# Delta rule in 32x32 blocks: the inversion on 128 GpSimd partitions, sent by GpSimd itself and joined by 32x32 matmuls

## The chip, the cores and the metric

One Trainium2 chip, one core of it. The metric is device time in microseconds of one execution; the median of three executions is given. The profile is one execution taken by the hardware profiler.

## What is computed

The program is a three-layer network over 512 tokens. The change lies in the first layer's mixer, which runs three attention groups and a gated delta rule (8 heads of width 128) beside each other. The delta rule as the reference has it, cut to what matters here:

```python
a_mat = jnp.where(tril_strict, jnp.einsum('nbhid,nbhjd->nbhij', kbeta, kc) * decay_mat, 0.0)
t_mat = lax.linalg.triangular_solve(eye + a_mat, eye, left_side=True, lower=True, unit_diagonal=True)
u = jnp.einsum('nbhij,nbhjd->nbhid', t_mat, vc * bc[..., None])
w = jnp.einsum('nbhij,nbhjd->nbhid', t_mat, kbeta * jnp.exp(gcum)[..., None])
```

The kernel works with chunks of 128 tokens, so each head has four strictly triangular 128x128 matrices, and the inverse of (1 + a) is wanted for each.

## The kernel before

All large products are made in three matmuls from a high and a low part of both operands (`gemm`, line 295), 24 matmuls of 128x512 for a slab of weights. A slab is loaded by SP (line 278) and split by ScalarE (`whi`, line 282) and VectorE (`wlo`, line 286).

`first_mixer` (from line 912) weaves two streams: the eight heads of the delta rule (`dn_head`) and the attention (`attention`, twelve pairs and four mixes). Both are generators; each `yield x` says how much TensorE work, in planned units, was just written. `interleave` always continues the stream that is least far along relative to its total, `DN_T` for the heads and `AT_T` for the attention. Within the heads, the second half of head h-1 is interleaved with the first half of head h, once the three convolutions of head h are written (`heads`). Head 0's second half thus stands among head 1's first half, and head 7's second half stands beside attention alone. This gives the program order; the framework's scheduler makes each engine's order from it at build time, and an engine then runs its instructions strictly in that order. `tc.issue_after(self.last_mm.ins)` keeps the transposes of `t_` (line 587) behind the last large matmul written before them. After the mixer comes `branch`, whose `pB` products need all eight heads.

The part of a head that matters, with its lines:

- Line 540: GpSimd scales `dec`. Line 551: VectorE makes `at`, the transposed triangular matrices of the four chunks, 128x512.
- Lines 560 to 577: the diagonal 16x16 blocks are inverted. SP writes `at` to `blk[0]` in HBM (one DMA) and reads 32 diagonal blocks back, one block on each of 32 partitions (four DMAs). GpSimd runs forward substitution, 15 steps of a product and a subtraction (lines 571 and 573). SP writes the result to the diagonal of `blk[1]` (four DMAs), which was zeroed once, and reads the whole as `t_` (one DMA).
- Line 587: TensorE transposes `t_`, ScalarE copies it to `tt` (line 588).
- Lines 590 to 598: two levels join 16 to 32 and 32 to 64. Each level takes a masked `at` from GpSimd (`xm`, line 555), four 128x128 products (line 547), a copy by ScalarE (line 593), four more products, a subtraction by VectorE (line 595), four transposes (line 496) and a copy by ScalarE (line 597).
- Lines 600 to 610: the last level joins 64 to 128 with 64x64 products on parts of the array (lines 603 and 609).
- Then `kbe`, the recurrence over four chunks, the output norm and the gate. GpSimd multiplies the gate in (line 668). In `attn_mix` GpSimd adds up the groups (line 851).

An fp32 product is two instructions on TensorE in the profile, so four products show as x8; a transpose is one.

Of the kernel before, what the change touches and what calls it, by code (L numbers as in the profile page):

```python
# [22 lines left out]
F32 = mybir.dt.float32  # L23
# [8 lines left out]
P = 128  # L32
# [3 lines left out]
NEG = -1.0e30  # L36
MAGIC = float(0x5F3759DF)

DN_T, AT_T = 280.0, 251.0
DN2 = "cy", "at", "aq", "qd", "kbe", "ktl", "bv"  # L40
S5_T = 150.0
L0_POOL = 10
L0_T = 142.0, 88.0
AHEAD = 90
LEAD = (0, 1)
NR = 6
N0, SK = 4, 2
# [30 lines left out]
def _consts():  # L78
    p = np.arange(P)
    f = np.float32  # L80
    eye = (p[:, None] == p[None, :]).astype(f)
    neg = lambda ok: np.where(ok, f(0), f(NEG)).astype(f)
    c = {}
    c["ident"] = eye
    c["m_up"] = neg(p[:, None] <= p[None, :])
    c["m_lo"] = neg(p[:, None] >= p[None, :])
    c["m_prev"] = neg(p[None, :] >= p[:, None])
    c["m_res"] = neg((p[:, None] // 32 == p[None, :] // 32) & (p[:, None] >= p[None, :]))
    c["tri"] = (p[:, None] <= p[None, :]).astype(f)
    c["half"] = (p[:, None] // 64 == np.arange(2)[None, :]).astype(f)  # L90
    for i in range(7):
        b = 1 << i
        ok = (p[:, None] // (2 * b) == p[None, :] // (2 * b)) & (p[:, None] // b % 2 == 0) & (p[None, :] // b % 2 == 1)
        c[f"lv{i}"] = ok.astype(f)
    x = np.arange(3 + 512)
    c["un1"] = (x[None, :] - 3 == 4 * p[:, None]).astype(f)
    x = np.arange(12 + 512)
    c["un2"] = (x[None, :] - 12 == 16 * (p[:, None] % 32) + p[:, None] // 32).astype(f)
    return c


# [117 lines left out]
class Kern:  # L219
# [230 lines left out]
        self.hb = t("hb")  # L450
        nc.vector.tensor_scalar(self.hb, self.beta, 0.5, None, op0=OP.mult)

    @staticmethod
    def diag(t, c):

        a = t[:, c * P : (c + 1) * P]
        return bass.AP(a.tensor, a.offset, [[16 * S + 16, 8], [S, 16], [1, 16]])

    def dn_head(self, h):

        nc, dl, pa = self.nc, self.dl, self.pa
# [1 line left out]
        def T(tag, dt=F32):  # L463
            return dl.tile([P, S], dt, tag=tag, name=tag, bufs=2 if tag in DN2 else 1)
# [4 lines left out]
        def c4(x):  # L469
            return x.rearrange("p (c n) -> p c n", c=4)  # L470
# [22 lines left out]
        def tokmajor(x):  # L493
            ps = ptile("tmps")
            for c in range(4):
                nc.tensor.transpose(ps[:, c * P : (c + 1) * P], x[:, c * P : (c + 1) * P], self.ident)
            return ps
# [45 lines left out]
        def per_chunk(lhs, rhs):  # L543
            ps = ptile("pcps")
            for c in range(4):
                t = slice(c * P, (c + 1) * P)
                nc.tensor.matmul(ps[:, t], lhs[:, t], rhs[:, t], start=True, stop=True)  # L547
            return ps
# [1 line left out]
        at, aq = T("at"), T("aq")  # L550
        nc.vector.tensor_mul(at, per_chunk(sk, kb), dec)
        yield 0.9
        def masked(i):
            x = T("xm")
            nc.gpsimd.tensor_tensor(c4(x), c4(at), self.mb[f"lv{i}"][:, None, :].to_broadcast([P, 4, P]), op=OP.mult)  # L555
            return x


        blk, eng = self.blk[h % 2], self.sub_engine
        nc.sync.dma_start(blk[0], at)  # L560
        x = self.sm.tile([P, S], F32, tag="sq", name="sub", bufs=2)
        lm = dl.tile([32, 64], F32, tag="lm", name="lm")
        La, Lt = (x[0:32, i * 256 : (i + 1) * 256].rearrange("p (i k) -> p i k", k=16) for i in range(2))
        for c in range(4):
            nc.sync.dma_start(La[8 * c : 8 * c + 8], self.diag(blk[0], c))
        eng.memset(Lt, 0.0)
        eng.memset(x[0:32, 256:512:17], 1.0)
        for j in range(15):
            n, w = 15 - j, j + 1
            m = lm[0:32, 0 : n * w].rearrange("p (i k) -> p i k", k=w)  # L570
            eng.tensor_tensor(m, La[:, j, j + 1 :][:, :, None].to_broadcast([32, n, w]),
                              Lt[:, j, 0:w][:, None, :].to_broadcast([32, n, w]), op=OP.mult)
            eng.tensor_sub(Lt[:, j + 1 :, 0:w], Lt[:, j + 1 :, 0:w], m)
        for c in range(4):
            nc.sync.dma_start(self.diag(blk[1], c), Lt[8 * c : 8 * c + 8])
        tt, t_ = T("tt"), T("t")
        nc.sync.dma_start(t_, blk[1])
        nc.vector.tensor_mul(aq, per_chunk(sk, sq_), dec)
        yield 0.9
        rowmul(qd, sq_, [self.egc[:, c, h : h + 1] for c in range(4)])  # L580
# [2 lines left out]
        nc.vector.tensor_tensor(c4(bv), c4(pv), colb(self.hb), op=OP.mult)  # L583
        yield 0.5
        yield None
        with self.tc.issue_after(self.last_mm.ins):
            ps = tokmajor(t_)
        nc.scalar.copy(tt, ps)
        yield 0.2
        for i in (4, 5):  # L590
            x = masked(i)
            y = T("ty")
            nc.scalar.copy(y, per_chunk(x, t_))
            yield 0.9
            nc.vector.tensor_sub(tt, tt, per_chunk(y, tt))
            yield 0.9
            nc.scalar.copy(t_, tokmajor(tt))
            yield 0.2

        a, b = slice(0, 64), slice(64, 128)  # L600
        ps = ptile("pcps")
# [41 lines left out]
        ot = self.ob[h]  # L643
        nc.scalar.copy(ot, po)
        self.dump(f"o_raw{h}", ot)
        q2 = T("xm")
        nc.scalar.activation(q2, po, AF.Square)
        yield 1.5
        v = dl.tile([P, 4], F32, tag="ov", name="ov")
# [15 lines left out]
        nc.vector.tensor_mul(z, ps, self.rb)  # L665
        nc.scalar.activation(th, z, AF.Tanh, scale=0.5)
        nc.vector.scalar_tensor_tensor(z, th, 1.0, z, op0=OP.add, op1=OP.mult)
        nc.gpsimd.tensor_tensor(ot, ot, z, op=OP.mult)
        yield 5.4


# [137 lines left out]
    def attn_mix(self, j):  # L809

        nc, at, pa = self.nc, self.at, self.pa
        ms = [self.stat[0]]
        for g in (1, 2):

            ps = pa.tile([4, S], F32, tag="aa", name="unps", bufs=2)
            for b in range(4):
                nc.tensor.transpose(ps[:, b * P : (b + 1) * P], self.stat[g][:, b].rearrange("p a h -> p (a h)"), self.ident)
            row = at.tile([4, S], F32, tag="unr", name="unr")
            nc.scalar.copy(self.perm(row, g), self.as_perm(ps, g))
            ps = pa.tile([P, 4, 4], F32, tag="aa", name="unpt", bufs=2)  # L820
            for b in range(4):
                nc.tensor.transpose(ps[:, b, :], row[:, b * P : (b + 1) * P], self.ident[0:4, 0:4])
            t = at.tile([P, 4, 2, 2], F32, tag=f"mst{g}", name=f"mst{g}")
            nc.vector.tensor_copy(t.rearrange("p n a h -> p n (a h)"), ps)
            ms.append(t)
        yield 0.8
        mm = at.tile([P, 4, 2], F32, tag="mm_", name="mm_")
        nc.vector.tensor_tensor(mm, ms[0][:, :, 0], ms[1][:, :, 0], op=OP.max)
        nc.vector.tensor_tensor(mm, mm, ms[2][:, :, 0], op=OP.max)
        es, zz = [], at.tile([P, 4, 2], F32, tag="zz", name="zz")  # L830
        for g in range(3):
            e = at.tile([P, 4, 2], F32, tag=f"es{g}", name=f"es{g}")
            nc.vector.tensor_tensor(e, ms[g][:, :, 0], mm, op=OP.subtract)
            nc.scalar.activation(e, e, AF.Exp)
            es.append(e)
            if g == 0:
                nc.vector.tensor_tensor(zz, e, ms[g][:, :, 1], op=OP.mult)
            else:
                t = at.tile([P, 4, 2], F32, tag="zt", name="zt")
                nc.vector.tensor_tensor(t, e, ms[g][:, :, 1], op=OP.mult)  # L840
                nc.vector.tensor_add(zz, zz, t)
        nc.vector.reciprocal(zz, zz)
        oa = at.tile([P, S], F32, tag="unr", name="oa")
        for g in range(3):
            nc.vector.tensor_mul(es[g], es[g], zz)
            ps = self.half_rows(at, es[g].rearrange("p b e -> p (b e)"))
            if g == 0:
                nc.vector.tensor_mul(oa, self.on[g], ps)
            else:
                nc.vector.tensor_mul(self.on[g], self.on[g], ps)  # L850
                nc.gpsimd.tensor_add(oa, oa, self.on[g])
            yield 0.2
        self.dump(f"oa{j}", oa)
        self.split(oa, self.oah[j], self.oal[j])
# [57 lines left out]
    def first_mixer(self):  # L912
        nc, tc = self.nc, self.tc
        with ExitStack() as c0:
# [4 lines left out]
            with ExitStack() as c1:  # L919
# [22 lines left out]
                    nc.scalar.dma_start(t, self.I["consts"][:, o : o + w])  # L942
                    return t

                for n in ("m_up", "m_res", "m_lo", "m_prev", "lv4", "lv5"):
                    self.mb[n] = dk.tile([P, P], BF, name="b" + n)
                    nc.gpsimd.tensor_copy(self.mb[n], load(n))
                for n in ("tri",):
# [3 lines left out]
                self.on = [at.tile([P, S], F32, name=f"on{g}") for g in range(3)]  # L952
                self.stat = [at.tile([P, 4, 2, 2], F32, name=f"stat{g}") for g in range(3)]
                dram = c1.enter_context(self.pool("blk", 1, bass.MemoryType.DRAM))
                self.blk = [[dram.tile([P, S], F32, name=f"blk{i}{j}") for j in range(2)] for i in range(2)]
                z = self.sm.tile([P, S], F32, tag="sq", name="zsq")
                nc.gpsimd.memset(z, 0.0)
                for i in range(2):
                    nc.scalar.dma_start(self.blk[i][1], z)
                self.sub_engine = nc.gpsimd  # L960
                self.cin = self.dl.tile([P, S + 4], F32, name="cin")
                nc.gpsimd.memset(self.cin[:, 0:4], 0.0)
                self.gqk = at.tile([P, 1], F32, name="gqk")
# [1191 lines left out]
```

## Time and profile before

| | |
|---|---|
| median of 3 runs | 2258.52 us (2255.84 to 2261.11) |
| the profiled execution | 2258.31 us |
| its span, first to last instruction | 2256.5 us |
| mean granted TensorE clock | 0.983 |
| TensorE busy | 2143.0 us, 95% |
| VectorE busy | 1487.9 us, 66% |
| ScalarE busy | 966.1 us, 43% |
| GpSimd busy | 442.5 us, 20%, 616 instructions |

The span is the time from the first to the last instruction on the core; 1.8 us of the execution lie around it. Matmuls overlap in the pipeline, so busy time of TensorE says only when it had something in flight; what a group of matmuls costs is read from the distance of starts.

### The profile page before, as it was taken

How to read it: one execution, taken by the hardware profiler on the slowest of the kernel's cores; microseconds unless marked ns; L12 is line 12 of the kernel's file. 1: busy time of each engine (PE TensorE's matmuls, PEld its weight loads, DVE VectorE, ACT ScalarE, POOL GpSimd, SP SyncE). 2: the span in 40 equal slices, each digit the busy share in tenths (PEclk: the TensorE clock that was granted, in tenths of full speed). 3: DMA queues.
4: the chain of work that ended last, by engine and by line, in shares of the span. 5: the costliest groups of instructions: out<-in, count | busy, mean ns of one | idle time of the engine just before them, and what ended most of it. 6: DMA issues, size and time to landing. Idle time of an engine off the chain costs nothing.

```text
span 2256.5 us, 28801 instructions
## 1 busy us (share of the span) xinstructions
PE 2143.0 (95%) x10718; PEld 1701.1 (75%) x10718; DVE 1487.9 (66%) x2674; ACT 966.1 (43%) x1594; POOL 442.5 (20%) x616
## 2 busy tenths in 40 slices
PE   8999999999999998999897899999999889999997
PEld 6787777777777886665785677788888778888886
DVE  6766766766755456775789878847476567777533
ACT  4434444444443233665464454424334245444321
POOL 0222022022020013101236059600330220000000
PEclk9999999999999998999998999999999999999998
DMA  4221111211212246899221112222232113322332
GB/s 158 67 68 52 67 62 49 80 63 58 72 39 89 92 159 228 305 356 310 89 95 47 29 49 92 94 94 97 84 103 94 47 38 103 103 94 96 96 95 88
DMA packets 83298, 231.13 MB, mean 102 GB/s; under 512 B 18576, under 2 KB 22288, under 8 KB 83152
## 3 DMA queue, kind: packets, MB, share of 16 engines
q1 hardware_dynamic: 78048, 217.02, 29.0%
q0 software_dynamic: 2944, 10.49, 1.4%
q10 hardware_dynamic: 2160, 1.71, 0.3%
q8 instruction: 86, 1.41, 0.3%
q14 instruction: 60, 0.49, 0.1%
HBM read 215.89 MB, written 12.65 MB: 101 GB/s over the span
## 4 chain that ended last, share of the span: by engine, by line
PE 40%; DVE 8%; ACT 2%; issue 1%; POOL 0%; DVEq 0%; POOLq 0%; ACTq 0%
PE mm L295 35%; DVE cvps L1711 2%; DVE wlo L286 1%; DVE fy L1787 1%; PE po L1662 1%; PE psc L1631 0%; PE st L1489 0%; PE gps L1935 0%; PE ppt L1655 0%; ACT whi L282 0%; DVE x L888 0%; DVE t L2044 0%; PE mm L2005 0%; DVE xl L306 0%; PE mm L2006 0%
## 5 line engine op out<-in xcount | busy, mean ns | idle before, releaser
L295 PE MATMUL mm<-xh,whi 128*128 128x512 f32 x1664 | 661.0, 398 | 13.4 <-ACT whi L282 12.9
L295 PE MATMUL mm<-xh,wlo 128*128 128x512 f32 x1664 | 660.3, 397 | 9.3 <-DVE wlo L286 9.2
L295 PE MATMUL mm<-xl,whi 128*128 128x512 f32 x1664 | 659.4, 396 | 7.0 <-DVE xl L303 3.9
L282 ACT CAST whi<-wraw 128x1024 fp32r<-128x1024 f32 (+4 forms) x311 | 301.4, 969 | 518.7 <-PE mm L295 421.7
L286 DVE TENSOR_TENSOR wlo<-wraw,whi 128x1024 fp32r<-128x1024 f32 (+4 forms) x311 | 367.6, 1182 | 127.0 <-ACT whi L282 123.6
L295 PEld LDWEIGHTS mm<-xh,wlo 128*128 128x128 f32 x1664 | 314.7, 189 | 78.3 <-DVE wlo L286 14.8
L295 PEld LDWEIGHTS mm<-xh,whi 128*128 128x128 f32 x1664 | 314.5, 189 | 77.4 <-ACT whi L282 14.2
L295 PEld LDWEIGHTS mm<-xl,whi 128*128 128x128 f32 x1664 | 314.8, 189 | 75.8 <-DVE xl L306 8.0
L1787 DVE SCALAR_TENSOR_TENSOR fy<-fe,par,fy 128x512 f32<-128x512 f32 x176 | 142.0, 807 | 4.0 <-ACT fy L1785 0.9
L295 PE MATMUL mm<-ah,whi 128*128 128x512 f32 x352 | 138.0, 393 | 0.2 <-ACT ah L302 0.2
L295 PE MATMUL mm<-al,whi 128*128 128x512 f32 x352 | 137.3, 391 | 0.0
L295 PE MATMUL mm<-ah,wlo 128*128 128x512 f32 x352 | 137.2, 390 | 0.0
L1782 DVE TENSOR_TENSOR fe<-mm,rb 128x512 f32<-128x512 f32 x88 | 60.3, 688 | 72.0 <-PE mm L295 69.2
L295 PEld LDWEIGHTS mm<-ah,whi 128*128 128x128 f32 x352 | 66.0, 188 | 15.7 <-ACT ah L302 1.5
L295 PEld LDWEIGHTS mm<-al,whi 128*128 128x128 f32 x352 | 66.1, 188 | 14.2 <-DVE al L303 0.4
L295 PEld LDWEIGHTS mm<-ah,wlo 128*128 128x128 f32 x352 | 66.1, 188 | 14.2
L1785 ACT ACTIVATE fy<-fe,par 128x512 f32<-128x512 f32 x88 | 71.9, 817 | 9.6 <-DVE fe L1782 8.9
L302 ACT CAST ah<-fy 128x512 fp32r<-128x512 f32 x44 | 27.4, 623 | 112.6 <-DVE fy L1791 112.5
L1803 DVE TENSOR_TENSOR x<-x,mm 128x512 f32<-128x512 f32 x32 | 22.0, 688 | 79.7 <-PE mm L295 79.7
L555 POOL TENSOR_TENSOR xm<-at,blv 128x512 f32<-128x512 f32 x16 | 19.5, 1222 | 247.0 <-PE pcps L547 201.6
L1124 DVE TENSOR_TENSOR xl<-wraw,xh 128x1024 fp32r<-128x1024 f32 x40 | 48.9, 1223 | 24.6 <-ACT xh L1123 24.0
L1790 ACT ACTIVATE fy<-fy 128x512 f32<-128x512 f32 x44 | 27.9, 634 | 84.9 <-DVE fy L1787 84.9
(746 smaller groups left out, 3646.3 us busy)
## 6 DMA issues: line engine op xcount, KB each, us to landing
wraw<-in_w_up SPq DMA_DIRECT2D x88, 512.0 KB
wraw<-in_w_eu SPq DMA_DIRECT2D x64, 512.0 KB
wraw<-in_w_dn SPq DMA_DIRECT2D x48, 512.0 KB
wraw<-in_w_qkv SPq DMA_DIRECT2D x36, 512.0 KB
wraw<-in_w_ed SPq DMA_DIRECT2D x32, 512.0 KB
wraw<-in_w_g SPq DMA_DIRECT2D x16, 512.0 KB
wraw<-in_w_l SPq DMA_DIRECT2D x16, 512.0 KB
wraw<-in_w_dn SPq DMA_DIRECT2D x16, 448.0 KB
```

What stands on the lines that cost most here:

```text
L282: nc.scalar.copy(hi, raw)
L286: nc.vector.tensor_sub(lo, raw, hi.bitcast(F32))
L295: self.last_mm = nc.tensor.matmul(ps, w, x, start=first and n == 0, stop=last and n == tot - 1)
L302: nc.scalar.copy(hi, src)
L1124: (nc.gpsimd if self.ncv < 5 else nc.vector).tensor_sub(lo, raw, hi.bitcast(F32))
L1662: nc.tensor.matmul(po[:, e, :], pts[e][:, c * P : (c + 1) * P], v1[:, c, h * 64 : h * 64 + 64], start=c == 0, stop=c == b)
L1711: nc.vector.scalar_tensor_tensor(yp, u[:, j : j + S], w(j), yp, op0=OP.mult, op1=OP.add)
L1782: nc.vector.tensor_mul(e[:, 2:], ps, self.rb)
L1785: nc.scalar.activation(y, e[:, 2:], AF.Identity, scale=w(2), bias=self.V(f"l{i}_fcb", f))
L1787: nc.vector.scalar_tensor_tensor(y, e[:, t : t + S], w(t), y, op0=OP.mult, op1=OP.add)
L1790: nc.scalar.activation(c[0], c[0], AF.Silu)
L1803: nc.vector.tensor_add(self.x[m], self.x[m], ps)
```

## The change

A 32x32 block is inverted where a 16x16 block was. GpSimd works on 128 partitions: 16 blocks, eight partitions for each, four rows on a partition. It runs 31 steps of a product and a subtraction on 128 x 4 x i elements, i from 31 down to 1. The blocks go to HBM in eight DMAs of SP and come back in two, each block's columns repeated for its eight partitions; a start matrix (`rows4`) is loaded by SP. The result is written to HBM and read into the diagonal blocks of `t_` by five DMAs that GpSimd itself issues; `t_` is now two fixed tiles, zeroed once. The masked level 16 to 32 goes away. The level 32 to 64 is made of 32x32 products: eight, a copy by ScalarE, and twelve, with results taken from two PSUM banks. The two GpSimd multiplications of lines 668 and 851 go to VectorE; line 540 stays. `DN_T` is 257, and heads 0 and 7 write `yield HOLD` (1.5 units) ahead of the transposes of `t_`.

```diff
-DN_T, AT_T = 280.0, 251.0
+DN_T, AT_T = 257.0, 251.0
+HOLD = 1.5
...
+    c["rows4"] = (x[None, :] % 32 == 4 * (p[:, None] % 8) + x[None, :] // 32).astype(f)
...
-        def masked(i):
-            x = T("xm")
-            nc.gpsimd.tensor_tensor(c4(x), c4(at), self.mb[f"lv{i}"][:, None, :].to_broadcast([P, 4, P]), op=OP.mult)
-            return x
-        blk, eng = self.blk[h % 2], self.sub_engine
-        nc.sync.dma_start(blk[0], at)
-        x = self.sm.tile([P, S], F32, tag="sq", name="sub", bufs=2)
...
-        for c in range(4):
-            nc.sync.dma_start(La[8 * c : 8 * c + 8], self.diag(blk[0], c))
...
-        for j in range(15):
...
-        for c in range(4):
-            nc.sync.dma_start(self.diag(blk[1], c), Lt[8 * c : 8 * c + 8])
-        tt, t_ = T("tt"), T("t")
-        nc.sync.dma_start(t_, blk[1])
+        ab, tb = self.blk[h % 2]
+        eng = self.sub_engine
+        for b in range(4):
+            for i, n in ((1, 32), (0, 16)):
+                o = 32 * b + 16 * i
+                nc.sync.dma_start(bass.AP(ab.tensor, ab.offset + 8192 * i + 64 * n * b, [[16, n], [16 * n, 4], [1, 16]]),
+                                  c4(at)[32 * b : 32 * b + n, :, o : o + 16])
+        La = [None, None]
+        for i, n in ((1, 32), (0, 16)):
+            la = self.sm.tile([P, S], F32, tag="sq", name="la", bufs=2)
+            nc.sync.dma_start(la[:, 0 : 16 * n], bass.AP(ab.tensor, ab.offset + 8192 * i, [[16 * n, 16], [0, 8], [1, 16 * n]]))
+            La[i] = la.rearrange("p (k i) -> p k i", i=16)
+        x = dl.tile([P, 2, P], F32, tag="sub", name="sub")
+        nc.sync.dma_start(x[:, 0, :], self.I["consts"][:, _COFF["rows4"][0] : _COFF["rows4"][0] + P])
+        Lt = x[:, 0, :].rearrange("p (r k) -> p r k", r=4)
+        for i in range(31, 0, -1):
+            m = x[:, 1, 0 : 4 * i].rearrange("p (r k) -> p r k", r=4)
+            eng.tensor_tensor(m, La[i // 16][:, 0:i, i % 16][:, None, :].to_broadcast([P, 4, i]),
+                              Lt[:, :, i][:, :, None].to_broadcast([P, 4, i]), op=OP.mult)
+            eng.tensor_sub(Lt[:, :, 0:i], Lt[:, :, 0:i], m)
+        t_ = self.t_[h % 2]
+        nc.gpsimd.dma_start(tb, x[:, 0, :])
+        for b in range(4):
+            nc.gpsimd.dma_start(c4(t_)[32 * b : 32 * b + 32, :, 32 * b : 32 * b + 32],
+                                bass.AP(tb.tensor, tb.offset + 4096 * b, [[32, 32], [1024, 4], [1, 32]]))
...
         yield None
+        if h in (0, 7):
+            yield HOLD
+        tt, y = T("tt"), T("ty")
         with self.tc.issue_after(self.last_mm.ins):
             ps = tokmajor(t_)
         nc.scalar.copy(tt, ps)
         yield 0.2
-        for i in (4, 5):
-            x = masked(i)
-            y = T("ty")
-            nc.scalar.copy(y, per_chunk(x, t_))
-            yield 0.9
-            nc.vector.tensor_sub(tt, tt, per_chunk(y, tt))
-            yield 0.9
-            nc.scalar.copy(t_, tokmajor(tt))
-            yield 0.2
+        lo, hi = (slice(0, 32), slice(64, 96)), (slice(32, 64), slice(96, 128))
+        ps = [ptile("pcps") for _ in lo]
+        for c in range(4):
+            for p in range(2):
+                nc.tensor.matmul(c4(ps[p])[hi[p], c, 0:32], c4(at)[lo[p], c, hi[p]], c4(t_)[lo[p], c, lo[p]], start=True, stop=True)
+        for p in range(2):
+            nc.scalar.copy(c4(y)[hi[p], :, 0:32], c4(ps[p])[hi[p], :, 0:32])
+        yield 0.3
+        ps = [ptile("pcps") for _ in lo]
+        for c in range(4):
+            nc.tensor.matmul(c4(ps[0])[hi[0], c, 32:64], c4(tt)[hi[0], c, hi[0]], c4(y)[hi[0], c, 0:32], start=True, stop=True)
+            for p in range(2):
+                nc.tensor.matmul(c4(ps[p])[lo[p], c, 0:32], c4(y)[hi[p], c, 0:32], c4(tt)[hi[p], c, hi[p]], start=True, stop=True)
+        nc.scalar.mul(c4(t_)[hi[0], :, 0:32], c4(ps[0])[hi[0], :, 32:64], -1.0)
+        for p in range(2):
+            nc.vector.tensor_scalar(c4(tt)[lo[p], :, hi[p]], c4(ps[p])[lo[p], :, 0:32], -1.0, None, op0=OP.mult)
+        yield 0.5
...
-        nc.gpsimd.tensor_tensor(ot, ot, z, op=OP.mult)
+        nc.vector.tensor_tensor(ot, ot, z, op=OP.mult)
...
-                nc.gpsimd.tensor_add(oa, oa, self.on[g])
+                nc.vector.tensor_add(oa, oa, self.on[g])
...
-                for n in ("m_up", "m_res", "m_lo", "m_prev", "lv4", "lv5"):
+                for n in ("m_up", "m_res", "m_lo", "m_prev"):
...
-                z = self.sm.tile([P, S], F32, tag="sq", name="zsq")
-                nc.gpsimd.memset(z, 0.0)
-                for i in range(2):
-                    nc.scalar.dma_start(self.blk[i][1], z)
+                self.t_ = [self.dl.tile([P, S], F32, name=f"t{i}") for i in range(2)]
+                for t in self.t_:
+                    nc.gpsimd.memset(t, 0.0)
```

## Rows read from the trace of the kernel before

**Rows 1.** Busy us by window (PE, PEld, DVE, ACT, POOL), granted clock, DMA share, GB/s.

```profile
60.00:700.00 640.00, 616.81 (x3684) 491.45 (x3685) 424.40 (x996) 275.51 (x588) 128.65 (x295) 1.00 0.19 62
700.00:750.00 50.00, 50.00 (x219) 40.72 (x218) 24.16 (x24) 14.51 (x19) 3.86 (x3) 1.00 0.28 90
```

**Rows 2.** PE's largest wait, 60 to 700 us: total, times, longest.

```profile
PE rowps L267 <- DVE f L519: 10.1, 8, 1.8
```

**Rows 3.** PE, a product of the two levels, 60 to 700 us: busy, mean ns, idle.

```profile
L547 PE MATMUL pcps<-t,xm 128*128 128x128 f32 x128 | 18.4, 283 | 0.0
```

**Rows 4.** PE in order of time, 274 to 291 us: start, duration, instruction.

```profile
275.88 1.06 PE L547 MATMUL pcps<-kb,sk 128*128 128x128 f32 x8
276.69 0.48 PE L295 MATMUL mm<-xh,whi 128*128 128x512 f32 x1
277.00 0.39 PE L295 MATMUL mm<-xl,whi 128*128 128x512 f32 x1
...
277.91 0.63 PE L496 MATMUL tmps<-ident,tt 128*128 128x128 f32 x4
278.29 0.48 PE L295 MATMUL mm<-xl,whi 128*128 128x512 f32 x1
...
289.02 0.40 PE L295 MATMUL mm<-xh,whi 128*128 128x512 f32 x1
289.36 0.67 PE L603 MATMUL pcps<-t,at 64*64 64x64 f32 x8
289.96 0.50 PE L295 MATMUL mm<-xl,whi 128*128 128x512 f32 x1
290.30 0.40 PE L295 MATMUL mm<-xh,wlo 128*128 128x512 f32 x1
```

**Rows 5.** Head 0 in order of time, from `at` to the transposes of `t_`.

```profile
75.93 0.69 DVE L551 TENSOR_TENSOR at<-pcps,dec 128x512 f32<-128x512 f32 x1 [0.49 <-POOL dec L540]
...
76.65 0.33 SPq L560 DMA_DIRECT2D blk<-at  x1
...
79.22 1.40 SPq L565 DMA_DIRECT2D sub<-blk  x4
...
82.31 0.21 POOL L571 TENSOR_TENSOR lm<-sub 32x15 f32<-32x15 f32 x1 [3.12 <-DMA sub<-blk]
...
95.68 0.21 POOL L573 TENSOR_TENSOR sub<-sub,lm 32x15 f32<-32x15 f32 x1
...
98.73 0.34 SPq L577 DMA_DIRECT2D t<-blk  x1
...
106.45 0.60 PE L496 MATMUL tmps<-ident,t 128*128 128x128 f32 x4
```

**Rows 6.** Head 7 in order of time, from `at` to the 64x64 products.

```profile
613.53 0.69 DVE L551 TENSOR_TENSOR at<-pcps,dec 128x512 f32<-128x512 f32 x1 [0.35 <-PE mm L295]
...
620.87 0.21 POOL L571 TENSOR_TENSOR lm<-sub 32x15 f32<-32x15 f32 x1 [7.38 <-DMA sub<-blk]
...
631.93 0.21 POOL L573 TENSOR_TENSOR sub<-sub,lm 32x15 f32<-32x15 f32 x1
...
643.99 0.66 PE L496 MATMUL tmps<-ident,t 128*128 128x128 f32 x4
...
659.84 0.68 PE L603 MATMUL pcps<-t,at 64*64 64x64 f32 x8
```

**Rows 7.** A wide step of the substitution, in order of time.

```profile
211.71 0.31 POOL L573 TENSOR_TENSOR sub<-sub,lm 32x64 f32<-32x64 f32 x1
```

**Rows 8.** DMAs that GpSimd issues in a later stage, as a group.

```profile
L1270 POOL DMA_INDIRECT big<-h2d,ti x16 | 17.0, 1063 | 132.8 <-PE mm L1409 109.1 <-DVE ovt L1228 10.3 <-DVE hw L1273 8.1
```

**Rows 9.** What SP's queue waited for, 50 to 700 us: total, times, longest.

```profile
SPq L575 <- POOL sub L573: 63.3, 8, 14.0
```

**Rows 10.** Head 1, `dec` on GpSimd and the transposes of `t_`, in order of time.

```profile
114.49 1.04 POOL L540 TENSOR_TENSOR dec<-dec,rqk 128x512 f32<-128x512 f32 x1 [4.63 <-ACT dec L539]
...
186.35 0.60 PE L496 MATMUL tmps<-ident,t 128*128 128x128 f32 x4
```

More of the change, by code (lines that the diff above doesn't have):

```diff
@@ L98, in _consts @@
     c["un2"] = (x[None, :] - 12 == 16 * (p[:, None] % 32) + p[:, None] // 32).astype(f)
+    x = np.arange(P)
+    c["rows4"] = (x[None, :] % 32 == 4 * (p[:, None] % 8) + x[None, :] // 32).astype(f)
     return c
@@ L451, in dn_scalars @@
         nc.vector.tensor_scalar(self.hb, self.beta, 0.5, None, op0=OP.mult)
[L453 to L457, printed above, removed]
     def dn_head(self, h):
@@ L552, in dn_head @@
         yield 0.9
-        def masked(i):
-            x = T("xm")
-            nc.gpsimd.tensor_tensor(c4(x), c4(at), self.mb[f"lv{i}"][:, None, :].to_broadcast([P, 4, P]), op=OP.mult)
-            return x
-        blk, eng = self.blk[h % 2], self.sub_engine
-        nc.sync.dma_start(blk[0], at)
-        x = self.sm.tile([P, S], F32, tag="sq", name="sub", bufs=2)
-        lm = dl.tile([32, 64], F32, tag="lm", name="lm")
-        La, Lt = (x[0:32, i * 256 : (i + 1) * 256].rearrange("p (i k) -> p i k", k=16) for i in range(2))
@@ L564, in dn_head @@
-        for c in range(4):
-            nc.sync.dma_start(La[8 * c : 8 * c + 8], self.diag(blk[0], c))
-        eng.memset(Lt, 0.0)
-        eng.memset(x[0:32, 256:512:17], 1.0)
-        for j in range(15):
[L569 to L573, printed above, removed]
@@ L645, in dn_head @@
         self.dump(f"o_raw{h}", ot)
-        q2 = T("xm")
+        q2 = T("ty")
         nc.scalar.activation(q2, po, AF.Square)
@@ L954, in first_mixer @@
                 dram = c1.enter_context(self.pool("blk", 1, bass.MemoryType.DRAM))
-                self.blk = [[dram.tile([P, S], F32, name=f"blk{i}{j}") for j in range(2)] for i in range(2)]
-                z = self.sm.tile([P, S], F32, tag="sq", name="zsq")
-                nc.gpsimd.memset(z, 0.0)
-                for i in range(2):
-                    nc.scalar.dma_start(self.blk[i][1], z)
+                self.blk = [[dram.tile([P, P], F32, name=f"blk{i}{n}") for n in (0, 1)] for i in range(2)]
                 self.sub_engine = nc.gpsimd
+                self.t_ = [self.dl.tile([P, S], F32, name=f"t{i}") for i in range(2)]
+                for t in self.t_:
+                    nc.gpsimd.memset(t, 0.0)
                 self.cin = self.dl.tile([P, S + 4], F32, name="cin")
```

## The prediction

> **What bounds the kernel now.** I read the table of windows first. From 60 to 700 us, where heads and attention are woven, TensorE is busy 616.8 of 640 us at a granted clock of 1.00; VectorE has 424, ScalarE 276, GpSimd 129, and the DMA engines 19% [rows 1]. Next I read TensorE's waits there: the largest is 10.1 us in eight pieces, for a small VectorE chain that the change leaves alone [rows 2]. So at most 23 us of this stage are idle, and the stage gets shorter by what TensorE no longer has to issue. Behind it TensorE is busy 50 of 50 us with 219 large matmuls, 0.228 us each [rows 1]; what follows the mixer is only moved earlier. Last I followed heads 0 and 7 in order of time, since the result of GpSimd's substitution has least room there [rows 5, 6].
>
> **What leaves TensorE.** Durations overlap, so I count distances of starts. Four 128x128 products (x8) stand 0.81 us before the next large matmul, and that one then takes 0.31 to its successor and not 0.228: 0.89 us a group, 0.101 for each instruction inside [rows 4]. The two levels have four such groups a head (128 instructions in 8 heads for the first product of both levels, and as many for the second) [rows 3]: 3.56 us. Four transposes take 0.38 plus the same 0.08, twice: 0.92 us [rows 4]. A head loses 4.48 us, eight heads 35.8 us.
>
> **What TensorE gets.** Eight and twelve 32x32 products, 40 instructions a head. No row shows one. The nearest is the 64x64 group: 0.60 us for eight, 0.075 each; with both neighbours, 289.02 to 290.30 less two steps of 0.228, it costs 0.82, so 0.22 lies around the group [rows 4]. The ends for a 32x32 instruction: half of 0.075, if it goes by columns, is 0.037; the 0.101 of a 128-wide one is the most. I take 0.05, nearer the row it is next to than a full halving, because consecutive ones use different rows and columns of the array. With two times 0.22 around: 2.44 us a head, 19.5 in all (ends 1.92 and 4.48, so 15.4 and 35.8). TensorE saves 35.8 - 19.5 = 16.3 us, with ends 20.4 and 0.
>
> The 0.22 us around a 64x64 group, against 0.08 around a 128x128 one, speaks against small tiles [rows 4]. [...]
>
> **VectorE and ScalarE.** VectorE loses sixteen 128x512 subtractions and gets sixteen 128x512 products or sums from lines 668 and 851, at 0.69 us like `at` [rows 5]: 11 us each way, and it idles 216 of 640 us [rows 1]. ScalarE loses four copies a head and gets two or three narrower ones. Nothing; if their cover went, both would still be no busier than now. The masks, their loads and the zeroing of HBM at the start go, two memsets come, all on GpSimd and ScalarE's queue ahead of the first `dec`: nothing.
>
> **GpSimd and its queue.** A substitution step took 0.21 us for 15 elements and 0.31 for 64 [rows 5, 7]: 0.18 us plus 2.0 ns an element. The old 30 instructions have 1360 elements, 8.1 us; they took 11.3 in head 7 and 13.6 in head 0 [rows 5, 6], so 0.105 to 0.18 us an instruction go between and beside them. The new 62 have 3968 elements: 19.1 us plus 6.5 to 11.3, so 25.6 to 30.4; I take 27, as head 7 is closer to an undisturbed one. This is 16 us a head more, beside TensorE.
>
> [...]
>
> Before GpSimd starts: 5.7 us from the end of `at` to the first step now. Eight stores at 0.35 us (1.40 for four) instead of one add 2.5, two loads instead of four take off 0.7 [rows 5]: 7.4 us. The `rows4` load needs nothing of `at`. After GpSimd: now 2.8 us to the issue of `t_` and about 2.6 to land, the time from the store of `at` to the loads that wait for it [rows 5]; 5.4. GpSimd's own DMAs cost it 1.06 us each to issue in another stage [rows 8]: 1.06, 2.6 to land, 4 x 1.06 and 2.6: 10.4 us (ends 5.4 and 10.4). From `at` to `t_` it was 24.7 us and will be 44.8, with ends 38.4 and 48.2.
>
> SP's queue is passed: the four stores that waited 63 us for GpSimd, with weight loads behind them, leave it [rows 9]. That gains nothing while no large wait of TensorE is for weights [rows 2]. GpSimd's queue now holds `dec` of the next head behind these 45 us. Between head 1 and later ones there are 70 us or more from `dec` to the use of `t_` (114.5 to 186.4) [rows 10], so six heads hide it all. What shows is at heads 0 and 7.
>
> **Heads 0 and 7.** `t_` was there at 101.3 and used at 106.45 in head 0; head 7 used it at 644.0, 29.8 us after `at` [rows 5, 6]. The 531 planned units fill some 640 us, 1.2 us a unit. `HOLD` puts 1.5 units of head 1 and 2.9 of attention ahead in head 0, 5.3 us, and 1.5 units in head 7, 1.8 us. So `t_` is 121.4 - 111.8 = 9.6 us late in head 0 and 659.0 - 645.8 = 13.2 in head 7. On the other side, the two levels took 15.8 us from the transposes to the 64x64 products [rows 6]; the new one has 2.4 us of products and three short copies, some 5.5. What follows in head 7 is thus about 3 us late. In head 0 GpSimd also comes to `dec` of head 1, now at 114.5, only some 3 us later [rows 10]. TensorE's order already lays other work between dependent groups (a 15.8 us chain with 4.5 us of work in it cost next to no idle time [rows 2, 6]), so I take 5 us of idle time for both heads; ends 0 and, if nothing lies in between, 9.6 + 13.2 = 23.
>
> **Sum.** -16.3 + 5 = -11.3 us against the profiled execution's 2258.3 (span 2256.5 plus 1.8 around it; the median of the runs is 0.2 above it): **2247 us**.
>
> **Rivals.** First, cheap products and no new wait: 0.037 us an instruction and `t_` covered: -20.4, 2238 us. For it: small parts of the array overlap; TensorE's few waits now. Against: 0.22 us around each group does not shrink. Second, nothing to be seen: 32x32 products cost as much as 128-wide ones (0 saved), or waits of 12 to 20 us take the saving back: 2254 to 2262 us, written as 2258. For it: 64x64 ones cost three quarters of 128-wide ones, not a half. Third, slower: TensorE stands at the transposes of `t_` in heads 0 and 7 for the whole lateness, 23 us for 16.3 saved: +6.7, 2265 us. It decides where the order holds less than 16 us of other work ahead of them in both heads together. For it: the arithmetic of the last part, with five DMAs in a row on GpSimd. Against: `HOLD` is a handle for just this place, and products of the next stage, which need no head, can fill head 7.
>
> **Chances.** Forecast 0.50, first rival 0.22, second 0.16, third 0.12. Within 0.2%, or 4.5 us, is what a measurement can hardly tell from no change. Faster by more: 0.50 + 0.22 = 0.72; same 0.16; slower 0.12. The range runs from just below the first rival, 2236, to the upper part of the second, 2261; it leaves out the third and a little below.
>
> **What would show it.** Head 7's 64x64 products should start near 649 us instead of 659.8 [rows 6], with TensorE's idle time up to there some 5 us above what it was. In the groups, 16 and 24 small products with starts 0.05 apart show the saving right; 0.1 apart shows it wrong. Sixty-two steps of GpSimd in 25.6 to 30.4 us, and `t_` landing some 45 us after `at`, show the lateness. A wait of TensorE's transposes for a DMA of 5 us or more in heads 0 and 7 shows the third rival; idle time elsewhere in the weave, on `dec` above all, would make the prediction wrong in a way not counted here.

## The result, and the profile after

The changed kernel takes **2298.22 us** (median of 4 runs, 2297.67 to 2299.41), the kernel before in the same comparison 2257.72 us: a ratio of 1.0174 (95% interval 1.016 to 1.0187). The forecast was 2247 us, with a range up to 2261. It is slower by 40 us; the profiled execution has a span of 2295.9 us.

The table of windows says where. Each row is a stretch, with the busy time of PE, PEld, DVE, ACT and POOL, the granted clock, the DMA share and GB/s. The stretch runs from 60 us to the first product of the stage behind the weave: 682.15 us before, 722.84 us after. The kernel before:

```profile
60.00:682.00 622.00, 598.89 (x3607) 477.09 (x3608) 411.82 (x980) 267.91 (x576) 127.35 (x294) 1.00 0.19 62
```

The changed kernel:

```profile
60.00:722.00 662.00, 592.34 (x3604) 463.17 (x3605) 409.30 (x997) 259.13 (x570) 229.47 (x544) 0.95 0.18 59
```

The weave is 40.7 us longer; what follows takes 1573.1 us where it took 1574.4. TensorE idles 662 - 592.3 = 69.7 us instead of 23.1, and its busy time has hardly fallen, at a clock of 0.95 instead of 1.00. So 46.6 us of new idle time are the first thing to explain. TensorE's waits (total, times, longest) answer to [rows 2]:

```profile
PE tmps L493 <- DMA t<-blk: 21.6, 2, 14.2
PE orps L270 <- DVE ory L667: 8.3, 7, 3.4
PE hrow L699 <- ACT hx L696: 8.1, 2, 7.9
PE qst L736 <- ACT q L733: 8.1, 3, 7.6
PE po L815 <- ACT pt L804: 7.3, 1, 7.3
PE mm L298 <- ACT whi L285: 6.9, 2, 6.6
```

Two kinds are new. One is the wait for `t_`, twice. The other is a single long stop in each of four groups, always for ScalarE: 7.58, 7.29, 6.59 and 7.95 us before 263.43, 349.31, 434.16 and 606.05 us, 29.4 us in all. Both kinds together are 51.0 us; the small waits got 4.4 us shorter.

**The four stops.** One of them, followed back through three engines. TensorE in order of time (start, duration, instruction, idle before it):

```profile
263.43 1.11 PE L736 MATMUL qst<-ident,q 128*128 128x128 f32 x4 [7.58 <-ACT q L733]
```

ScalarE did `q` (L733) late because the conversion of weights ahead of it in its order was late:

```profile
261.80 1.04 ACT L285 CAST whi<-wraw 128x1024 fp32r<-128x1024 f32 x1 [11.86 <-DMA wraw<-in_w_qkv]
262.75 0.63 ACT L733 ACTIVATE q<-k 128x512 f32<-128x512 f32 x1
```

Those weights were asked for at 257.73 us, right behind another load. SP's queue in order of time:

```profile
230.71 0.36 SPq L281 DMA_DIRECT2D wraw<-in_w_dn  x1
257.33 0.36 SPq L565 DMA_DIRECT2D sub<-in_consts  x1
257.73 0.43 SPq L281 DMA_DIRECT2D wraw<-in_w_qkv  x1
```

For 26 us SP issues nothing. It stands at L565, the load of `rows4` into `sub` for the *next* head. There is one `sub` tile; the load has to wait until the head before has left it, and the last to read it is GpSimd's store of its result (L573), issued at 255.39. SP's waits (total, times, longest), to set against [rows 9]:

```profile
SPq L565 <- DMA blk<-sub: 160.2, 7, 26.8
```

The other three stops go the same way: ScalarE's conversions at 347.72, 433.06 and 602.33 us had waited 7.7, 15.0 and 10.6 us for weights that SP asked for right behind the load of `rows4` at 343.34, 428.33 and 598.10. But not each of the seven waits stops TensorE. In order of time they are 22.4, 14.1, 26.2, 25.0, 23.4, 26.8 and 22.1 us; the third, fourth, fifth and seventh are the ones before the four stops. Behind the longest, which ended at 521.58, TensorE was still at work on weights it had, and stood for 0.30 us here and 0.53 us a little later:

```profile
526.55 0.50 PE L298 MATMUL mm<-xh,whi 128*128 128x512 f32 x1 [0.30 <-ACT whi L285]
```

So it is not the length of such a wait alone that decides, but also how much work TensorE has at that place before it needs the weights queued behind.

**`t_` in heads 0 and 7.** Head 0 in order of time, to set against [rows 5]. VectorE, then GpSimd:

```profile
74.25 0.69 DVE L548 TENSOR_TENSOR at<-pcps,dec 128x512 f32<-128x512 f32 x1 [0.15 <-PE pcps L544]
...
82.49 0.48 POOL L569 TENSOR_TENSOR sub<-la,sub 128x124 f32<-128x124 f32 x1 [9.53 <-DMA la<-blk]
...
114.12 0.20 POOL L571 TENSOR_TENSOR sub<-sub 128x4 f32<-128x4 f32 x1
114.63 0.79 POOL L573 DMA_DIRECT2D blk<-sub  x1 [0.31 <-POOL sub L571]
116.98 2.23 POOL L575 DMA_DIRECT2D t<-blk  x4 [1.55 <-DMA blk<-sub]
```

and TensorE:

```profile
123.13 1.09 PE L493 MATMUL tmps<-ident,t 128*128 128x128 f32 x4 [7.36 <-DMA t<-blk]
124.14 0.63 PE L598 MATMUL pcps<-t,at 32*32 32x32 f32 x8
...
125.30 0.63 PE L298 MATMUL mm<-xl,whi 128*128 128x512 f32 x1
125.73 0.63 PE L298 MATMUL mm<-xh,wlo 128*128 128x512 f32 x1
126.15 1.05 PE L802 MATMUL ppt<-ident,pe 128*128 128x128 f32 x4
127.14 0.44 PE L598 MATMUL pcps<-t,at 32*32 32x32 f32 x8
```

From the end of `at` to the use of `t_` are 48.2 us; head 7 has 14.19 us of waiting, and its transposes start at 689.67 instead of the 643.99 of [rows 6].

**The clock behind a stop.** In the rows above, two large matmuls start 0.43 us apart where 0.228 is usual, and four transposes take 1.09 instead of 0.60 us. Windows of the changed kernel around four of the stops, with an undisturbed one among them, and at the end the 10 us right behind the stop of head 7:

```profile
258.00:275.00 17.00, 11.57 (x45) 9.57 (x46) 10.28 (x23) 5.51 (x7) 1.99 (x4) 0.80 0.41 135
275.00:343.00 68.00, 64.28 (x413) 50.35 (x411) 43.30 (x102) 27.57 (x70) 27.36 (x64) 1.00 0.14 46
343.00:360.00 17.00, 10.38 (x56) 7.91 (x57) 8.63 (x24) 6.73 (x12) 2.17 (x4) 0.80 0.34 120
600.00:618.00 18.00, 11.95 (x56) 9.15 (x56) 9.63 (x20) 7.16 (x19) 0.76 (x2) 0.72 0.33 117
684.00:722.00 38.00, 28.92 (x176) 22.66 (x177) 15.44 (x51) 13.87 (x30) 2.42 (x5) 0.69 0.10 31
690.00:700.00 10.00, 10.00 (x80) 6.74 (x79) 2.51 (x15) 3.16 (x9) 0.00 (x0) 0.50 0.00 0
```

In the four windows with a stop the granted clock is 0.69 to 0.80, in the undisturbed one 1.00, and from 690 to 700 us, where TensorE is busy all the time, 0.50. Right behind the four stops it is 0.50 as well (264 to 266, 349 to 351, 434 to 436 and 606 to 608 us), and 1.00 again from 268 to 275, 353 to 360, 438 to 445 and 612 to 618 us. So a stop is paid for twice.

### The profile page after: what moved, and what is told of

It reads as the page before. It is cut to its first block, busy times and chain, and to the rows that moved or that the text cites. A ratio compares the mean times of both kernels' runs of the same rounds, so it can differ in the third digit from the quotient of the medians.

```text
span 2295.9 us, 29008 instructions
## 1 busy us (share of the span) xinstructions
PE 2134.7 (93%) x10718; PEld 1685.3 (73%) x10718; DVE 1485.0 (65%) x2690; ACT 954.4 (42%) x1586; POOL 543.2 (24%) x863
## 3 DMA queue, kind: packets, MB, share of 16 engines
q10 hardware_dynamic: 1584, 1.06, 0.2%
## 4 chain that ended last, share of the span: by engine, by line
PE 39%; DVE 8%; ACT 2%; issue 1%; POOL 0%; DVEq 0%; ACTq 0%; POOLq 0%
PE mm L298 35%; DVE cvps L1723 2%; DVE wlo L289 1%; DVE fy L1799 1%; PE po L1674 1%; PE psc L1643 0%; PE st L1501 0%; PE gps L1947 0%; ACT whi L285 0%; PE ppt L1667 0%; DVE t L2056 0%; PE mm L2017 0%; PE mm L2018 0%; PE mm L2019 0%; DVE x L900 0%
## 5 line engine op out<-in xcount | busy, mean ns | idle before, releaser
L298 PEld LDWEIGHTS mm<-xh,whi 128*128 128x128 f32 x1664 | 316.2, 190 | 86.9 <-ACT whi L285 23.1
L569 POOL TENSOR_TENSOR sub<-la,sub 128x124 f32<-128x124 f32 (+30 forms) x248 | 102.2, 412 | 102.5 <-DMA la<-blk 83.7
L571 POOL TENSOR_TENSOR sub<-sub 128x124 f32<-128x124 f32 (+30 forms) x248 | 96.4, 389 | 19.4
L537 POOL TENSOR_TENSOR dec<-dec,rqk 128x512 f32<-128x512 f32 x8 | 8.3, 1039 | 293.2 <-ACT dec L536 293.2
```

The costliest lines, as they stand in the source:

```text
L298: self.last_mm = nc.tensor.matmul(ps, w, x, start=first and n == 0, stop=last and n == tot - 1)
L569: eng.tensor_tensor(m, La[i // 16][:, 0:i, i % 16][:, None, :].to_broadcast([P, 4, i]), Lt[:, :, i][:, :, None].to_broadcast([P, 4, i]), o ...
L571: eng.tensor_sub(Lt[:, :, 0:i], Lt[:, :, 0:i], m)
```

## The experiments

Nine kernels, in three groups that each share the runs of the kernel before.

### 1. The start matrix stays in SBUF

```diff
-        nc.sync.dma_start(x[:, 0, :], self.I["consts"][...rows4...])
+        eng.tensor_copy(x[:, 0, :], self.r4)
```

`r4` is loaded once, ahead of the heads, by ScalarE's queue. Nothing else differs.

> The changed kernel, but the start matrix of the substitution is kept in SBUF and GpSimd copies it, so that no load stands in SP's queue waiting for the head before. Theory A (SP is held by the load of the start matrix, with weight loads behind it): the four stops of TensorE near 263, 349, 434 and 606 us, 29.4 us, go, and with them the half clock behind them, an estimate of 9 us from the four windows at a granted clock of 0.72 to 0.80; the two waits for t_ stay at about 21 us. 2298 - 38 = 2260 us, between 2254 and 2268. Theory B (GpSimd is too busy, and whatever waits for it is late in any case): the stops move elsewhere, 2290 us or more. Theory C (the small products or the order of the work cost the time): 2290 or more, with TensorE's busy time and not its idle time up.

Measured: **2257.84 us, ratio 0.9998 (0.9987 to 1.0008)**: the whole 40 us are gone, and it is the time of the kernel before. Window of this kernel, and its largest wait:

```profile
60.00:682.00 622.00, 584.88 (x3606) 459.33 (x3607) 410.95 (x997) 259.29 (x571) 236.75 (x551) 0.97 0.19 62
```

```profile
PE tmps L493 <- DMA t<-blk: 19.5, 2, 14.3
```

The four stops are gone, the two waits for `t_` have stayed, and no wait of SP for `sub` is left. Theory A holds, B and C fall: GpSimd works as long as before, and apart from the two waits for `t_` its 28 us a head hurt through the queue that stood behind it. Against the kernel before, busy time is 14.0 us less and idle time 14.0 us more (37.1 for 23.1).

### 2. A little more work ahead of `t_`

```diff
-DN_T, AT_T = 257.0, 251.0
+DN_T, AT_T = 272.0, 251.0
...
-            yield HOLD
+            yield 4.0 if h == 0 else 14.0
```

on top of the first.

> As the run before, and in addition more planned work ahead of the use of t_ in the first and the last head: 4 and 14 units where it was 1.5 each, with the planned total of the heads raised to 272. Theory A (t_ is simply used too early by the order): the two waits for t_, 21.6 us, fall under 5 us, and some 5 us of half clock go with them: 2235 to 2245 us. Rival: there is no other work left to lay in between in the last head, or what is laid there is missed elsewhere, since attention then ends earlier or later than the heads: within 5 us of the run before.

Measured: 2256.67 us, ratio 0.9987 (0.9975 to 0.9998). The rival's number came. This kernel's waits:

```profile
PE tmps L493 <- DMA t<-blk: 15.4, 1, 15.4
PE tmps L493 <- DVE at L548: 7.3, 1, 7.3
```

In head 7 nothing moved: from the end of `at` to the transposes there were 28.8 us of other work in the first experiment and 27.5 here. I read this as the planner having already filled the time for which it took GpSimd to be busy, so that my 14 units lay inside that. That is not shown; the fifth experiment rests on this reading. In head 0 one wait replaced another: `at` of head 1 needs its `dec`, and that stands behind the substitution on GpSimd.

### 3. Half of the substitution

```diff
-        for i in range(31, 0, -1):
+        for i in range(15, 0, -1):
```

The load of `rows4` is left where the change has it.

> The changed kernel with 15 of the 31 steps of the substitution: the 16 longest, which join the two halves of each 32x32 block, are left out. GpSimd then needs about 9 us a head where it needed 28, and everything that waits for it is some 18 us earlier. Theory A (lateness of GpSimd's result, through SP's queue and through t_): stops for weights and t_ nearly gone, TensorE's idle time from 60 us to the end of the stage back to 25 us or less, 2230 to 2240 us. Theory C (the products themselves or the new order): 2270 or more.

Measured: 2233.39 us, ratio 0.9888 (0.987 to 0.9907), as theory A said. One wait for `t_`, 6.2 us, is left, in head 7. SP still waits at the load, for less time:

```profile
SPq L565 <- DMA blk<-sub: 75.3, 7, 16.0
```

TensorE's longest idle times are now that wait and two of 3.2 and 1.9 us, none of them behind a weight load. So the same wait in the same queue costs nothing while it is 11 us a head on average and 16.0 at most, and 29.4 us of idle time when it is 23 and 26.8. That is how the 63.3 us of [rows 9], 14.0 at most, could be harmless. All the waits up to 16.0 us did no harm; above 22 us four of six did.

### 4. Only the join to 64x64 by small products, in the kernel before

```diff
-        for i in (4, 5):
+        for i in (4,):
...
+        y = T("ty")
+        ... # the two passes of 32x32 products, as in the change
```

> The kernel before, in which only the join of 32x32 blocks to 64x64 is done by 32x32 products; the substitution of 16x16 blocks and the masked join to 32x32 stay. Nothing gets later. It takes two groups of four 128x128 products and one of transposes off each head (2 x 0.89 + 0.46 = 2.24 us, 17.9 in all) and adds 40 small products. Theory A (small products cost what the trace of the changed kernel shows, 10.5 us in all): -7, 2248 to 2252 us. My prediction's size (0.05 each and 0.22 around each group, 19.5 us): +1.6, 2257 to 2261 us.

Measured: **2241.76 us, ratio 0.9923 (0.9906 to 0.9941)**: -17 us, more than either said.

```profile
60.00:667.00 607.00, 590.27 (x3772) 467.83 (x3770) 408.12 (x999) 268.77 (x590) 115.65 (x286) 1.00 0.20 63
```

Busy time falls by 8.6 us and idle time by 6.4, to 16.7. By distances of starts, what left TensorE is 18.3 us and the 320 small instructions take 6.4, which is cheaper still than in the changed kernel (10.5). The number of groups explains it: here they stand in 16 groups, in the changed kernel in 27, and a group takes about 0.4 us in both (see the last section). The 6.4 us less of idle time I had not foreseen; the waits for `f` fell from 10.1 to 5.8 us, and I did not test why.

### 5. Much more work ahead of `t_` in head 7

The diff of the second experiment with `1.5 if h == 0 else 30.0` and a total of 285.5.

> The start matrix in SBUF as before, and 30 planned units instead of 1.5 ahead of the use of t_ in head 7 alone (planned total 285.5). With 14 units the distance from at to the use of t_ in head 7 had stayed 28 us, so the planner had already laid that much there by itself, and 14 units added nothing. Theory A (t_ is 43 us behind at, the order gives it 28): with 30 units the order gives it over 40, the wait of 14.3 us in head 7 falls under 3, and the half clock behind it (0.89 and 0.83 in two stretches of 50 us) goes as well; head 0's 5.2 us stay. 2258 - 11 - 8 = 2239 us, between 2234 and 2245. Rival: what is laid in between is missing behind it, so that the chain of the last head stands bare: within 5 us of 2258.

Measured: **2239.42 us, ratio 0.9909 (0.9895 to 0.9923)**, the number expected.

```profile
60.00:663.00 603.00, 580.95 (x3603) 458.65 (x3604) 410.98 (x997) 256.69 (x569) 244.19 (x551) 0.98 0.20 63
```

Between the end of `at` and the transposes of head 7 TensorE now has 42.3 us of other work. Head 7's wait is 0.3 us, head 0's is 7.1. Idle time is back at 22.1 us; the clock is far below 1.00 only behind head 0's wait (0.67 from 110 to 135 us).

### 6. Somewhat more in head 0 as well

`6.0 if h == 0 else 30.0`, total 290, and `dec` of head 1 by VectorE:

```diff
-        nc.gpsimd.tensor_tensor(c4(dec), c4(dec), rk...)
+        (nc.vector if h == 1 else nc.gpsimd).tensor_tensor(c4(dec), c4(dec), rk...)
```

> As the run before, and 6 units instead of 1.5 in head 0 (planned total 290), with dec of head 1 multiplied by VectorE, since with 4 units in head 0 TensorE had waited 7.3 us for at of head 1, whose dec stands behind the substitution in GpSimd's queue. Theory A: head 0's wait of 5.2 us goes too and nothing takes its place: 3 to 8 us below the run before. Rival: head 0's t_ is still waited for, since the planner already lays there what there is: within 2 us of the run before.

Measured: 2243.34 us, ratio 0.9933 (0.992 to 0.9947), 4 us above the run before: a miss for both. Head 0's wait fell from 7.1 to 4.5 us, but head 7 waits 3.5 us again. That a larger total leaves less attention for the same 30 units can account for 0.8 us of it at most: there are 41.5 us of other work where there were 42.3. The rest is `t_` itself, which came later: the transposes start 45.0 us behind the end of `at`, in the run before 42.6. Why was not tested.

### 7. SP sends instead of GpSimd

On top of the first experiment:

```diff
-        nc.gpsimd.dma_start(tb, x[:, 0, :])
+        nc.sync.dma_start(tb, x[:, 0, :])
...
-            nc.gpsimd.dma_start(c4(t_)...)
+            nc.sync.dma_start(c4(t_)...)
```

> The start matrix in SBUF, but the store of GpSimd's result and the four loads of t_ are issued by SP instead of GpSimd. Theory A (whatever waits for GpSimd in SP's queue holds the weight loads behind it, and 28 us are longer than the buffers cover): SP stands at the store for 20 us a head, and stops of TensorE for weights come back: 2275 to 2300 us. Rival (the stores of before waited 63 us in this queue at no cost, and GpSimd is spared four issues): 2250 to 2262 us.

Measured: **2316.73 us, ratio 1.0254 (1.0237 to 1.027)**; theory A's side, and 17 us beyond it. SP's wait is back, now at the store:

```profile
SPq L573 <- POOL sub L571: 177.3, 8, 25.0
```

and ScalarE waits for weights:

```profile
ACT whi L285 <- DMA wraw<-in_w_qkv: 54.3, 4, 15.4
```

It is the mechanism of the four stops made by another instruction; why it costs 17 us more than I expected was not taken apart. So the clause "GpSimd sends them itself" was not the harmless extra that I took it for: with a substitution of 28 us it is what keeps SP free, and the load of `rows4` gave that away.

### 8. GpSimd does the gate product and the sum again

On top of the first: lines 680 and 863 back on GpSimd.

> The start matrix in SBUF, but the gate product of a head and the addition to oa are GpSimd's again, as in the kernel before. Theory (both are needed late, and GpSimd has room): 2254 to 2264 us, as the kernel with the start matrix in SBUF. Rival (they stand behind up to 28 us of substitution in GpSimd's queue, and push dec and the next substitution back by as much as they take): 2265 us or more, with waits of TensorE or SP for oa.

Measured: 2275.73 us, ratio 1.0075 (1.0059 to 1.0092); the rival's side, some 18 us above the first experiment. From 60 us to the end of the weave (699.5) it has 10.6 us more idle time than that one and 6.4 more busy time at a lower clock, 0.96. GpSimd stood 26.3 us at one sum, waiting for ScalarE, with `dec` of the next head behind it; but that `dec` then waited for ScalarE in its turn:

```profile
190.81 3.85 POOL L863 TENSOR_TENSOR oa<-oa,on 128x512 f32<-128x512 f32 x2 [26.25 <-ACT hx L696]
212.20 1.04 POOL L537 TENSOR_TENSOR dec<-dec,rqk 128x512 f32<-128x512 f32 x1 [17.54 <-ACT dec L536]
```

So the sum did not push this `dec` back, and no wait of TensorE or SP for `oa` shows: the rival has the time right, but its mechanism is not shown. ScalarE waits 16.5 us in four pieces for these sums (8.1 us in three in the first experiment). What made the 18 us stays open. Which of the two operations did it was not tried apart.

### 9. More work in head 0 and head 7 together

`12.0 if h == 0 else 33.0`, total 299, `dec` of head 1 by VectorE, start matrix in SBUF.

> The start matrix in SBUF, 33 planned units ahead of the use of t_ in head 7 and 12 in head 0 (planned total 299), dec of head 1 by VectorE. With 6 units in head 0 the wait had only gone from 7.1 to 4.5 us and head 7 got 3.5 us back, since a larger total leaves less attention for its 30 units. Theory A (t_ is late by the length of the substitution, and enough work in the order hides it): head 0's wait goes below 1 us with the half clock behind it, head 7's stays below 2: 2228 to 2236 us. Rival (the work laid into head 0 and 7 is missing between the dependent steps of the other heads, whose small waits grow): 2238 us or more, with the waits for orps and rowps up.

Measured: **2230.39 us, ratio 0.9872 (0.9848 to 0.9895)**, the fastest of all.

```profile
60.00:654.00 594.00, 575.00 (x3605) 452.93 (x3605) 412.21 (x999) 256.20 (x568) 243.44 (x550) 1.00 0.20 64
```

```profile
PE orps L270 <- DVE ory L667: 9.7, 8, 2.0
PE tmps L493 <- DMA t<-blk: 1.4, 1, 1.4
```

The clock is 1.00 throughout and idle time 19.0 us. With both clocks at 1.00, this row also gives the price of the change in busy time: 598.9 - 575.0 = 23.9 us less work for TensorE.

## Why the prediction was wrong

With that price each kernel's weave adds up, against the kernel before, from the windows:

| us | work | slower clock | idle | weave |
|---|---|---|---|---|
| changed kernel | -23.9 | +17.3 | +46.6 | +40.0 |
| start matrix in SBUF | -23.9 | +9.9 | +14.0 | 0.0 |
| and 30 units in head 7 | -23.9 | +6.0 | -1.1 | -19.0 |
| and 12 and 33 units | -23.9 | 0 | -4.1 | -28.0 |

The column of the clock is what the busy time has above that of the last kernel, so its last entry is 0 by construction; it shrinks as the stops do.

- **The step that failed: "SP's queue is passed."** I said that the four stores leave SP's queue, that this gains nothing, and that the `rows4` load "needs nothing of `at`". The last is true, and it is the wrong question. The load needs the single `sub` tile, which GpSimd gives back only with its store at the end of the substitution. So SP's wait for GpSimd did not leave: it grew from 63.3 to 160.2 us, with the weight loads still behind it. The first experiment shows it (2298 to 2258 us by that one line); the seventh brings it back in another form. In the text I had asked of the new load what it reads, and not what it overwrites. A second `sub` tile might have freed SP as well; it was not run.
- **"That gains nothing while no large wait is for weights."** The 63 us of [rows 9] in eight pieces cost nothing, and I took that for a property of the queue. It was one of the length and the place: the third experiment has 75 us in seven pieces without a stop, and in the changed kernel, with pieces of 22 to 27 us, four of six stopped TensorE.
- **Heads 0 and 7: mis-sized.** I took 5 us of idle time, with ends 0 and 23. The waits are 21.6 us. The place and the upper end were right, and so was the third rival's price of 23; its sum of 2265 lacked the stops. What I held against it, that `HOLD` and other work fill the place, did not hold: 1.5 units left 14 us uncovered in head 7, and the fifth experiment needed 30.
- **The lower clock behind a stop was in no term**: 17.3 us in the changed kernel by the table, more than the 16.3 that I had counted as the whole saving.
- **What leaves TensorE:** 35.8 us, by distances of starts it is 37.3. Right.
- **What TensorE gets:** 19.5 us, ends 15.4 and 35.8; measured 10.5 in all, outside the ends. The 10.5 run from start to start; my 0.22 around a group also held what the next large matmul is longer, about 0.1 us, so with it some 13, still outside. The term that was wrong is the 0.05 us for each instruction: at a granted clock of 1.00 a group takes 0.36 to 0.38 us to the next start, whether it has 8, 16 or 24 (last section). By busy time the saving is 23.9 us instead of 16.3, so even the first rival's 20.4 was too low; by distances of starts it is 37.3 - 10.5 = 26.8, and where the 2.9 between the two lie stays open.
- **VectorE and ScalarE, nothing:** right for the change as it is, since VectorE's busy time stays at 409 to 412 us. What I did not see is that the two operations on GpSimd cost 18 us, as the eighth experiment has it.
- **GpSimd:** 27 us for the substitution, ends 25.6 and 30.4; it took 31.8 in head 0, 28.2 in head 1 and 27.8 in head 7. So head 0 lies 1.4 us above the upper end, and the other two between the ends. In head 0, from `at` to its start 7.4 us were forecast and 7.5 measured; from its end to the use of `t_` 10.4 and 8.8; in all 44.8 and 48.2, the upper end, since what was too short behind the substitution made up in part for what was too long in it. The four loads of `t_` took GpSimd 2.2 us to issue and not 4.2: the row that I took the 1.06 us from is of indirect DMAs [rows 8]. The lateness as a whole was right.
- **The stride.** The forecast's sum has no term for it. A product of the changed kernel reads a column with a step of 64 bytes; it takes 0.46 us for 124 elements where the subtraction takes 0.43, and the means of all 248 are 412 and 389 ns. In the kernel before, whose products read no column, the two means are 306 and 302 ns. The 23 ns between product and subtraction are 6% of the whole instruction; of the part that grows with the elements, 23 ns of some 123 are about 19%, an estimate from 1.9 ns an element (0.20 us for 4, 0.43 for 124) and 64 elements on average. How much of the 23 ns is the step was not taken apart.
- **"Six heads hide it all"** holds for `t_`: only two waits for it show. It did not hold for what else waited on those six heads' GpSimd, and that was the risk I had named only for `dec`.

## What to carry to other kernels

When a change makes one engine's step more than twice as long, list every instruction on every in-order queue that waits for the end of that step, and among them those that wait only to overwrite a buffer; then name what is queued behind each. Here all such waits in SP's queue up to 16.0 us were harmless, and of six between 22.1 and 26.8 us four stopped TensorE, with a stretch at a granted clock of 0.50 on top; I read the limit as the lead that the loads ahead of the wait give at that place. And before calling work "hidden", see whether the order was laid with the new duration: here the same change went from +40 to -29 us by keeping a 64 KB constant resident, by telling the order how late the result comes, and with one `dec` moved to VectorE.

## What the runs showed of the hardware

32x32 products start much closer together than I expected. The second pass of head 0, at a granted clock of 1.00, in order of time:

```profile
130.36 0.21 PE L604 MATMUL pcps<-ty,tt 32*32 32x32 f32 x1
130.36 0.22 PE L606 MATMUL pcps<-tt,ty 32*32 32x32 f32 x2
130.41 0.19 PE L604 MATMUL pcps<-ty,tt 32*32 32x32 f32 x1
...
130.61 0.20 PE L606 MATMUL pcps<-tt,ty 32*32 32x32 f32 x2
130.73 1.16 PE L544 MATMUL pcps<-sq,sk 128*128 128x128 f32 x8
```

24 of them are started between 130.36 and about 130.61 us, 11 ns apart on average, and the next group starts 0.37 us after the first of them. The eight of a group of the first pass are 36 ns apart on average (above, at 127.14 us). Where all sixteen of the first pass stand together, as in head 3, they take no longer:

```profile
376.21 0.44 PE L598 MATMUL pcps<-t,at 32*32 32x32 f32 x16
376.58 0.50 PE L298 MATMUL mm<-xh,whi 128*128 128x512 f32 x1
376.91 0.39 PE L298 MATMUL mm<-xl,whi 128*128 128x512 f32 x1
```

There they start in pairs, 7 ns apart within a pair and 32 ns from pair to pair; the 24 of the second pass start in threes (one of line 604, two of line 606), 7 ns apart within a three and again 32 ns from one to the next. So at a granted clock of 1.00 a group of 8, of 16 or of 24 takes 0.363 to 0.369, 0.370 and 0.376 to 0.378 us to the next start in the changed kernel, and what counts is the number of groups. Eight 128x128 instructions took 0.81 us to the next start and eight 64x64 ones 0.60 [rows 4]; these 24 are cheaper than either.
